# MLP products of a two-layer trunk by Strassen's seven products instead of eight, with the hidden layer kept in DRAM

## The chip, the cores and the metric

The kernel runs on one core of one Trainium2 chip, as one launch. The metric is device microseconds of that core, the median of several runs. An engine name in a profile stands for one of the core's engines: PE is TensorE's matmuls, PEld its weight loads, DVE is VectorE, ACT is ScalarE, POOL is GpSimd, SP is SyncE, which issues most DMAs. "q" behind a name is that engine's instruction queue.

## What is computed

Two layers of a trunk work on 640 tokens (128 context, 512 latent) of 1024 channels in float32. In each layer three branches (a short gated convolution, differential attention, a convolution module) are merged and projected; then comes the squared-ReLU MLP, which this change is about:

```python
    x = x + gt1 * rmsnorm(m @ lw["w_o"], lw["g_post_mix"])
    h = rmsnorm(x, lw["g_pre_mlp"]) * (1 + sc2) + sh2
    f = jnp.square(jax.nn.relu(h @ lw["w_ff1"])) @ lw["w_ff2"]
    x = x + gt2 * rmsnorm(f, lw["g_post_mlp"])
```

w_ff1 is 1024 x 4096 and w_ff2 is 4096 x 1024. Scales and shifts (sh2, sc2, gt2 and their like, six chunks of 1024 a layer) come from w_mod and two conditioning vectors. The outputs are y_prompt, y_sample and the context's new keys and values.

## The kernel before

**Tiles.** Channels stand on the 128 partitions, tokens along the free axis, so an activation is 8 tiles of 128 x 640 and the MLP's hidden layer is 32 of them. `U()` takes a working tile (51 of them, `NU`, each 655 float32 wide), `hl()` two. Tokens are cut into two halves of 320 (`HALF`) or, where one sub-layer ends and the next begins, into parts of 256 and 384 (`PART`).

**Split products.** Every float32 operand is split into a high part, rounded to fp32r, and a low part, the rest. A product is three matmuls: high by high, high by low, low by high. `wblock` loads a block of 128 x 1024 weights (tile `raw`, 3 of them), makes the high part on ACT (`wh`) and the low part (`wl`) by a subtraction that goes to DVE or POOL (`nc.either`); there are 5 such pairs (`NW`). `gemm` issues the three products for both halves of the tokens; `proj` gives them a PSUM tile `pp` of two banks, `proj_half` a tile `ps` of one bank.

**MLP.** The hidden channels come in chunks of 4, 8, 8, 8 and 4 tiles (`CHUNKS`, lines 1387 to 1436). In a chunk every hidden tile is one `proj` over 8 input tiles, then `relu2` (ReLU and square on ACT, square and low part on DVE or POOL); then each of the 8 output tiles is one `proj` over the chunk's tiles, added into `ya` on DVE. The first chunk is started by `first`, part by part of the tokens, inside `tail`, the function that ends a sub-layer; the last chunk is itself the `tail` of the MLP, with the norm and the residual. In layer 0 the loop also steps through `mods`, which makes modulation vectors with `modvec`: one `raw` load and four multiply-and-sum instructions of 128 x 512 on DVE for each of 56 tiles (chunk 5 of layer 0 and all six chunks of layer 1). Layer 0's own chunks 2 to 4 are made during its merge of the branches; layer 1 has nothing of the kind there.

**Order of the work.** The program is first recorded as a list of operations (`Recorder`). `rank` gives each a due time so that TensorE may go on without a pause, `schedule` lists every engine's operations with a cost model (`cost`, `LAT`, `pe_time`), and `emit` issues them in that order; so all instructions of the page carry line 517. Each engine works through its list in order. Tiles are taken from their pools in this order, too.

Of the kernel before, what the change touches and what calls it, by code (L numbers as in the profile page):

```python
# [31 lines left out]
CHUNKS = (4, 8, 8, 8, 4)  # L32
# [65 lines left out]
class View:  # L98
    """A view of a tile: what is done to its access pattern, and the elements that it covers."""
# [70 lines left out]
# microseconds from an operation's end to the start of one that waits for it, by the two engines  # L170
# [15 lines left out]
class Recorder:  # L186
    def __init__(self, nc):
# [6 lines left out]
        # operations for either of two engines  # L194
        self.either = Engine(self, "vector", "gpsimd")

    def cost(self, eng, method, outs, ins, kw, args):
        """microseconds that an engine is held."""
# [5 lines left out]
        if eng == "tensor":  # L204
# [9 lines left out]
            return c / 2400  # L214
# [11 lines left out]
        if eng == "gpsimd":  # L226
            if ALU.pow in (kw.get("op"), kw.get("op1")):
                return 0.1 + m * 0.2
            if method == "memset":
                return 0.1 + m / 900  # L230
            return 0.155 + m * 2.1e-3
        return 0.06

    def add(self, eng, method, args, kw, other=None):
# [9 lines left out]
        if eng == "sync":  # L244
            sz = (outs + ins)[0].shape
            nbytes = 4 * int(np.prod(sz))
# [11 lines left out]
        if nbytes:  # L258
            op.acts = ("dma", nbytes)
        if eng == "scalar":  # L260
# [51 lines left out]
    def rank(self):  # L312
        """priorities: the latest start that lets TensorE go on without a pause, in its order of the program."""
        t = 0.0
        for op in self.ops:
            if op.eng == "tensor":
                op.prio = t
                t += op.cols / 2400
# [12 lines left out]
        for op in reversed(self.ops):  # L331
            d = op.dur
            if op.eng == "sync":
                d = 1.3 + op.acts[1] / 360e3
            for u in op.users:
# [4 lines left out]
    def schedule(self):  # L340
        """the operations in the order of their starts."""
# [17 lines left out]
        # operations that use each tile, to know when it is free  # L359
# [25 lines left out]
        def soon(e, op, start):  # L385
            """whether a late operation should let one go first that is about to be ready."""
# [31 lines left out]
        def pe_time(op, t):  # L418
            """duration on TensorE, whose clock doubles after a tick of enough work."""
            left, w, t0 = op.cols, op.load / op.cols, t  # L420
            while left > 0.5:
                i = int(t / TICK + 1e-9)
                rate = 2400 if busy.get(i - 1, 0) >= BUSY else 1200
# [8 lines left out]
        while len(seq) < n:  # L432
# [48 lines left out]
            if e == "sync":  # L481
                gen[0] = max(start, gen[0]) + 0.65
                dma[0] = max(gen[0] + 0.65, dma[0]) + op.acts[1] / 360e3
                op.end = dma[0]
            else:
# [35 lines left out]
def trunk_kernel(ctx: ExitStack, tc: tile.TileContext, xT, crow, ccol, wmod, wmod0, win, wv, wa, wc, wattn, wo, wff1, wff2,  # L521
# [49 lines left out]
    # ---- constants  # L571
# [12 lines left out]
    # ---- weights  # L584
# [5 lines left out]
    def wblock(src, eng=None):  # L590
        r = raw_load(src)
        wh = wp.tile([P, KD * P], F32R, tag="wh", name=nm("wh"), bufs=NW)
        wl = wp.tile([P, KD * P], F32R, tag="wl", name=nm("wl"), bufs=NW)
# [3 lines left out]

    def gemm(outs, wb, rhs, ks, koff=0):
        """outs: [(psum ap, c0, c1)]; rhs[k] = (hi, lo)."""
# [31 lines left out]
    def first(wbs, rhs, hf):  # L631
        """products of four blocks with one part of the tokens, in step with the tiles of rhs."""
# [21 lines left out]
    def sums(ss, c0, c1, w, pos=None):  # L654
        """sums over channels, tokens on partitions; w: the column of 1/n for the mean."""
# [16 lines left out]
    # ---- per-token statistics: means over channels, or rsqrt of them and eps, to a broadcast  # L672
# [22 lines left out]
    def sq_acc(acc, src, a, b, first):  # L695
        """acc[:, a:b] (+)= src^2"""
# [29 lines left out]
    def residual(xs, m, sq, hf, need, part):  # L726
        """m = xs + m * rstd; returns the squares of the new m."""
# [12 lines left out]

    def split(t, hi, lo, eng=None):
# [3 lines left out]
    # ---- modulation  # L745
# [12 lines left out]
    def cond():  # L758
        """silu of the two conditioning rows, on every partition, in halves."""
# [7 lines left out]
    def modvec(l, st, j, cb):  # L767
        """chunk j of the modulation vectors, a tile at a time."""
# [27 lines left out]
    # ---- start: the first layer's scale and shift a tile at a time, each followed by its products  # L796
# [64 lines left out]
    for l in range(DEPTH):  # L861
# [6 lines left out]
        # ---- Conformer conv branch: gated input, first two channel tiles half by half  # L868
# [55 lines left out]
        # ---- lambda  # L924
# [12 lines left out]
        # ---- attention  # L937
# [38 lines left out]
        def rope(pt, out, scale):  # L976
            """rotary embedding of the latent part of a projection into out; returns the projection."""
# [17 lines left out]
        def k_head(hd):  # L995
            """keys: (high parts twice over the partitions for each map, low parts), and the context's as they are."""
# [12 lines left out]
        def q_head(hd):  # L1009
            """queries, scaled: for each map its high part on its own partitions and the low part on the others."""  # L1010
# [7 lines left out]
        def softmax(S, n, view, s0):  # L1018
            """S: two psum views [q, n keys]; returns s0 * (p0 - lam p1) as a tile, s0 the sum under p0."""
# [17 lines left out]
        def three(out, A, B, start, stop):  # L1037
            """out (+)= A.T @ B from (hi, lo) pairs."""
# [30 lines left out]
        def values(aa, ac, v, vc):  # L1069
            """weights @ v of the latent and the context queries, channels on partitions; s0 times the output."""  # L1070
# [24 lines left out]
        def subln(o, s0, hd):  # L1095
            """the output, and what its queries are to be scaled by: rsqrt of the mean square and eps, times s0."""
# [20 lines left out]
        # ---- short gated conv branch  # L1117
# [69 lines left out]
        # ---- modulation vectors that are needed later  # L1187
        def mods(js):
            if l == 0:
                cb = cond()  # L1190
                for j in js:
                    yield from modvec(l, st[l], j, cb)
# [16 lines left out]
        def pair(wsrc):  # L1209
            """a block holds the products of two channel tiles."""  # L1210
# [19 lines left out]
        # ---- layer norm and silu of the conv branch  # L1230
# [22 lines left out]
        # ---- attention output  # L1253
# [38 lines left out]
        # ---- output projection, residual, second norm  # L1292
# [265 lines left out]
```

## Time and profile before

| | |
|---|---|
| median of 3 runs | 2613.51 us (2612.6 to 2614.75) |
| span of the profiled execution, first to last instruction | 2606.3 us |
| what the median has beyond that span | 7.2 us |
| PE busy, PEld busy | 2527.0 us (97%), 2459.4 us (94%), 17092 instructions each |
| DVE, ACT, POOL busy | 1663.9 (64%), 991.9 (38%), 329.0 us (13%) |
| mean granted TensorE clock | 0.985 |

The profiled execution is known by its span alone. Busy is the union of an engine's instructions. Matmuls are pipelined, so their single durations overlap, and what one costs is read from the distance between starts.

### The profile page before, as it was taken

How to read it: one execution, taken by the hardware profiler on the slowest of the kernel's cores; microseconds unless marked ns; L12 is line 12 of the kernel's file. 1: busy time of each engine (PE TensorE's matmuls, PEld its weight loads, DVE VectorE, ACT ScalarE, POOL GpSimd, SP SyncE). 2: the span in 40 equal slices, each digit the busy share in tenths (PEclk: the TensorE clock that was granted, in tenths of full speed). 3: DMA queues.
4: the chain of work that ended last, by engine and by line, in shares of the span. 5: the costliest groups of instructions: out<-in, count | busy, mean ns of one | idle time of the engine just before them, and what ended most of it. 6: DMA issues, size and time to landing. Idle time of an engine off the chain costs nothing. (4 is left out here: it accounts for less than half of the span.)

```text
span 2606.3 us, 41673 instructions
## 1 busy us (share of the span) xinstructions
PE 2527.0 (97%) x17092; PEld 2459.4 (94%) x17092; DVE 1663.9 (64%) x2807; ACT 991.9 (38%) x1714; POOL 329.0 (13%) x218
## 2 busy tenths in 40 slices
PE   7999999999999999999989999999999999999998
PEld 7988899999999999999989888999999989999998
DVE  7699787954675886775468988787243363333325
ACT  4666553223334432222446566433232343222213
POOL 2122220001201010110012222101010020000001
PEclk9999999999999899999989999999999989999999
DMA  7322222341453554444323212123221322222231
GB/s 268 94 79 67 77 73 79 132 168 66 138 182 110 172 172 146 154 151 134 116 74 92 69 62 81 65 105 120 78 73 66 112 91 81 74 73 77 78 110 46
DMA packets 103779, 273.80 MB, mean 105 GB/s; under 512 B 13012, under 2 KB 35876, under 8 KB 103588
## 3 DMA queue, kind: packets, MB, share of 16 engines
q1 hardware_dynamic: 103588, 271.14, 30.8%
q8 instruction: 134, 2.20, 0.3%
q14 instruction: 57, 0.47, 0.1%
HBM read 244.83 MB, written 17.87 MB: 101 GB/s over the span
## 5 line engine op out<-in xcount | busy, mean ns | idle before, releaser
L517 PE MATMUL pp<-u,wh 128*128 128x320 f32 (+2 forms) x6560 | 1245.7, 310 | 13.9 <-DVE u L517 11.4
L517 PEld LDWEIGHTS pp<-u,wh 128*128 128x128 f32 x6560 | 1034.3, 189 | 17.9 <-DVE u L517 13.9
L517 PE MATMUL pp<-u,wl 128*128 128x320 f32 (+2 forms) x3280 | 764.6, 309 | 0.0
L517 PE MATMUL ps<-u,wh 128*128 128x320 f32 (+2 forms) x2912 | 664.6, 317 | 6.0 <-ACT u L517 5.3
L517 DVE TENSOR_TENSOR wl<-raw,wh 128x1024 fp32r<-128x1024 f32 x265 | 332.7, 1256 | 373.8 <-ACT wh L517 373.4
L517 PEld LDWEIGHTS pp<-u,wl 128*128 128x128 f32 x3280 | 555.6, 189 | 0.0
L517 ACT CAST wh<-raw 128x1024 fp32r<-128x1024 f32 x312 | 326.8, 1049 | 590.2 <-PE pp L517 366.9
L517 PEld LDWEIGHTS ps<-u,wh 128*128 128x128 f32 x2912 | 493.3, 191 | 16.8 <-issue 6.7
L517 PE MATMUL ps<-u,wl 128*128 128x320 f32 (+2 forms) x1456 | 456.7, 314 | 0.0
L517 DVE TENSOR_TENSOR u<-u,u 128x640 fp32r<-128x640 f32 (+8 forms) x356 | 279.4, 794 | 65.7 <-ACT u L517 52.1
L517 PEld LDWEIGHTS ps<-u,wl 128*128 128x128 f32 x1456 | 276.9, 190 | 0.0
L517 ACT ACTIVATE u<-pp 128x640 f32<-128x640 f32 (+3 forms) x124 | 79.8, 649 | 439.1 <-PE pp L517 427.7
L517 DVE CUSTOM_DVE_ANT_0 u<-raw,u 128x512 f32<-128x512 f32 x320 | 227.4, 758 | 27.6 <-DMA raw<-in_wmod_dram 25.8
L517 DVE SCALAR_TENSOR_TENSOR u<-u,par,u 128x640 f32<-128x640 f32 (+16 forms) x272 | 240.2, 891 | 3.8
L517 POOL TENSOR_TENSOR wl<-raw,wh 128x1024 fp32r<-128x1024 f32 x47 | 121.7, 2590 | 494.2 <-ACT wh L517 285.6
L517 DVE TENSOR_TENSOR u<-u,pp 128x640 f32<-128x640 f32 (+2 forms) x60 | 45.2, 754 | 182.3 <-PE pp L517 182.1
L517 ACT CAST u<-u 64x640 fp32r<-64x640 f32 (+1 forms) x152 | 110.4, 727 | 121.3 <-DVE u L517 107.1
L517 ACT ACTIVATE u<-u 128x640 fp32r<-128x640 f32 (+5 forms) x200 | 117.5, 600 | 83.6 <-DVE u L517 67.6
L517 POOL TENSOR_TENSOR u<-u,u 128x384 f32<-128x384 f32 (+4 forms) x59 | 88.7, 1514 | 431.8 <-ACT u L517 227.2
L517 ACT ACTIVATE u<-pp,mx 128x640 f32<-128x640 f32 x128 | 100.9, 793 | 72.4 <-DVE mx L517 72.1
L517 PE MATMUL ps<-wh,u 128*128 128x256 f32 x640 | 122.3, 286 | 1.8 <-ACT vo L517 1.8
L517 DVE TENSOR_TENSOR u<-ps,u 128x512 fp32r<-128x512 f32 (+4 forms) x192 | 92.1, 507 | 45.2 <-PE ps L517 23.1
(91 smaller groups left out, 1839.9 us busy)
## 6 DMA issues: line engine op xcount, KB each, us to landing
raw<-in_wff_dram SPq DMA_DIRECT2D x128, 512.0 KB, 3.3
raw<-in_win_dram SPq DMA_DIRECT2D x120, 512.0 KB, 3.3
raw<-in_wmod_dram SPq DMA_DIRECT2D x80, 512.0 KB, 3.3
u<-in_wmod_dram SPq DMA_DIRECT2D x32, 256.0 KB, 6.0
raw<-in_wv_dram SPq DMA_DIRECT2D x16, 512.0 KB, 3.2
u<-u SPq DMA_DIRECT2D x128, 64.0 KB, 2.0
raw<-in_wattn_dram SPq DMA_DIRECT2D x16, 512.0 KB, 3.2
raw<-in_wo_dram SPq DMA_DIRECT2D x16, 512.0 KB, 3.3
```

The source lines that it names most:

```text
L517: getattr(eng, m)(*[r(v) for v in a], **{x: r(v) for x, v in k.items()})
```

## The change

The first 4 and the last 4 hidden tiles of each layer stay as they were (`FD`, `FE`). The other 28 are made two at a time: two output tiles, pairs of input tiles and two halves of the tokens are a 2 x 2 by 2 x 2 block product, done with seven block products and sums of operands. `wseven` makes the seven weight operands from one or two `raw` blocks: three DVE sums, a high part each on ACT, a low part each by a subtraction on DVE, or, for products 1, 2 and 4 (`ADD`), by a negated copy on ACT onto which POOL's DMA adds the block from DRAM. `sums_of` and `pair_of` make the activations' operands. `seven` runs the products in the order of `ORDER`; bank A takes products 1, 6, 7 and 4 one upon the other, and is read after each, bank C takes 5 and 3, bank B takes 2. All 32 hidden tiles are written to DRAM (`fd`) and read back in groups of 8 (4 pairs) for the second product. The pools change: weights are 10 tiles of one tag (each holds two of 512 columns), two tiles `sum` are new, `NU` goes from 51 to 48. In layer 0's MLP `mods` makes 24 tiles (its chunk 5, layer 1's chunks 1 and 0), in layer 1's MLP 8 (chunk 5); layer 1's chunks 2 to 4 move to its own merge. The cost model's TensorE rate goes from 2400 to 2225 columns a microsecond.

```diff
-CHUNKS = (4, 8, 8, 8, 4)
-NU = 51
-NW = 5
+NU = 48
+NW = 10
 NRAW = 3
+NSUM = 2
+ORDER = (1, 5, 6, 2, 7, 3, 4)
+ADD = (1, 2, 4)
+FD = 4
+FE = 4
+NF = 32
...
+    def wseven(srcs, add):
+        n = len(srcs) * 2 * P
+        rs = [raw_load(x) for x in srcs]
+        ss = [wp.tile([P, KD * P], F32, tag="sum", name=nm("sum"), bufs=NSUM) for _ in srcs]
...
+        w11, w22, w12, w21 = (part(rs, i) for i in range(4))
+        nc.vector.tensor_add(two(ss[0][:, :2 * n]), two(rs[0][:, :2 * n]), w21[:, None, :].to_broadcast([P, 2, n]))
+        s3, s1, s2, s4 = (part(ss, i) for i in range(4))
+        nc.vector.tensor_add(s2, s3, w22)
+        nc.vector.tensor_add(s4, s2, w12)
+        loaded = {1: 0, 4: 1, 2: 2}
+        of = {1: w11, 2: w12, 3: s4, 4: w22, 5: s1, 6: s2, 7: s3}
+        out = {}
+        for i in ORDER:
+            w = wtile()
+            hi, lo = w[:, :n], w[:, n:2 * n]
+            nc.scalar.copy(hi, of[i])
+            if i in add:
+                nc.scalar.mul(lo, of[i], -1.0)
+                nc.gpsimd.dma_start(lo, part(srcs, loaded[i]), accum_op=ALU.add)
+            else:
+                nc.vector.tensor_sub(lo, of[i], f(hi))
+            out[i] = hi, lo
+        return out
...
-    def modulate(x, sq, G, B, h, hf):
+    def modulate(x, sq, G, B, h, hf, keep=None):
...
+                if keep is not None:
+                    nc.scalar.activation(keep[k][:, s:e], t[:, s:e], AF.Identity, bias=B[:, k, g:g + 1])
...
+    def sums_of(x0, x1):
+        ta, tb = U(), U()
+        nc.vector.tensor_sub(ta[:, :TH], x0[:, :TH], x0[:, TH:])
+        nc.vector.tensor_sub(ta[:, TH:], x1[:, TH:], x0[:, TH:])
+        nc.vector.scalar_tensor_tensor(tb[:, :TH], ta[:, :TH], -1.0, x1[:, TH:], op0=ALU.mult, op1=ALU.subtract)
+        nc.vector.scalar_tensor_tensor(tb[:, TH:], tb[:, :TH], -1.0, x1[:, :TH], op0=ALU.mult, op1=ALU.subtract)
+        out = []
+        for t in (ta, tb):
+            th = hl()
+            nc.scalar.copy(th[0], t)
+            nc.vector.tensor_sub(th[1], t, f(th[0]))
+            out.append(th)
+        return out
...
+    def pair_of(x0, x1, h0=None, h1=None):
+        if h0 is None:
+            t = U(F32R)
+            nc.scalar.copy(t[:, :TH], x0[:, :TH])
+            nc.vector.tensor_sub(t[:, TH:], x0[:, :TH], f(t)[:, :TH])
+            x11 = t[:, :TH], t[:, TH:]
+            h1 = hl()
+            nc.scalar.copy(h1[0], x1)
+            nc.vector.tensor_sub(h1[1], x1, f(h1[0]))
...
+    def product(o, i, W, X, start):
...
+            nc.tensor.matmul(o, wh[:, s], hi, start=start and q == 0, stop=False, skip_group_check=True)
+            nc.tensor.matmul(o, wh[:, s], lo, start=False, stop=False, skip_group_check=True)
+            nc.tensor.matmul(o, wl[:, s], hi, start=False, stop=last, skip_group_check=True)
...
+    def seven(W, X, y0, y1, fresh):
+        ac = PP()
+        A, C = ac[:, 0, :TH], ac[:, 1, :TH]
+        B = PS()[:, :TH]
...
+        def put(y, o):
+            if fresh:
+                nc.scalar.copy(y, o)
+            else:
+                nc.vector.tensor_add(y, y, o)
+        product(A, 1, W, X, True)
+        put(y11, A)
+        product(C, 5, W, X, True)
+        put(y22, C)
+        product(A, 6, W, X, False)
+        put(y12, A)
+        product(B, 2, W, X, True)
+        nc.vector.tensor_add(y11, y11, B)
+        product(A, 7, W, X, False)
+        nc.vector.tensor_add(y22, y22, A)
+        product(C, 3, W, X, False)
+        nc.vector.tensor_add(y12, y12, C)
+        product(A, 4, W, X, False)
+        if not fresh:
+            nc.vector.tensor_add(y21, y21, A)
+        return A
...
-        for cx, cn in enumerate(CHUNKS):
...
+        for i in range(FD):
+            t = U()
+            for hf in range(2):
+                a, b = PART[hf]
+                nc.scalar.activation(t[:, a:b], lead[hf][i], AF.Relu)
+            nc.scalar.activation(t, t, AF.Square)
+            nc.sync.dma_start(fd[i], t)
+        X = [pair_of(hv[2 * j], hv[2 * j + 1], h[2 * j], h[2 * j + 1]) for j in range(KD // 2)]
...
+        for mp in range(FD // 2, NF // 2):
+            W = wseven([wff1[l, 2 * mp + u] for u in range(2)], ADD)
+            y0, y1 = U(), U()
+            A = seven(W, X, y0, y1, True)
+            nc.scalar.activation(y0, y0, AF.Relu)
+            nc.scalar.activation(y0, y0, AF.Square)
+            nc.scalar.activation(y1[:, :TH], A, AF.Relu, scale=-1.0)
+            nc.scalar.activation(y1[:, TH:], y1[:, TH:], AF.Relu, scale=-1.0)
+            nc.scalar.activation(y1, y1, AF.Square)
+            nc.sync.dma_start(fd[2 * mp], y0)
+            nc.sync.dma_start(fd[2 * mp + 1], y1)
+            for _ in range(2):
+                next(mv, None)
...
+        ya = [U() for _ in range(KD)]
+        nu = (NF - FE) // 4
+        for u0 in range(0, nu, 2):
+            us = list(range(u0, min(u0 + 2, nu)))
+            X = [load_pair(2 * u + i) for u in us for i in range(2)]
+            for mp in range(KD // 2):
+                W = wseven([wff2[l, u0 * (KD // 2) + mp * len(us) + i] for i in range(len(us))], ADD)
+                A = seven(W, X, ya[2 * mp], ya[2 * mp + 1], u0 == 0)
+                if u0 == 0:
+                    nc.scalar.copy(ya[2 * mp + 1][:, :TH], A)
```

The last four hidden tiles are read back, split, and go through `tail` as before; there every second output tile is held negated, so its add becomes a subtraction. The weights of both products are laid out on the host in the new order of blocks.

## Rows read from the trace of the kernel before

**Rows 1.** The page's first part: busy us, share of the span, instructions.
```profile
PE 2527.0 (97%) x17092; PEld 2459.4 (94%) x17092; DVE 1663.9 (64%) x2807; ACT 991.9 (38%) x1714; POOL 329.0 (13%) x218
```
**Rows 2.** Busy time by stretch: attention, merge, MLP, MLP's end, of both layers.
```profile
core 0: us, PE busy (x) PEld busy (x) DVE busy (x) ACT busy (x) POOL busy (x), PEclk, DMA share, GB/s
54.00:449.00 395.00, 382.16 (x2632) 353.66 (x2631) 321.52 (x529) 218.57 (x444) 77.30 (x48) 1.00 0.24 76
449.00:778.00 329.00, 328.47 (x2253) 328.21 (x2252) 223.78 (x378) 97.45 (x118) 35.72 (x17) 1.00 0.39 136
...
855.00:1240.00 385.00, 383.05 (x2574) 382.08 (x2575) 281.48 (x597) 101.95 (x129) 37.05 (x20) 0.99 0.46 153
...
1340.00:1736.00 396.00, 381.42 (x2569) 352.33 (x2569) 319.16 (x508) 210.18 (x429) 75.16 (x48) 0.99 0.24 77
1736.00:2065.00 329.00, 328.81 (x2258) 328.55 (x2257) 159.72 (x182) 91.89 (x112) 25.98 (x11) 1.00 0.26 88
...
2143.00:2165.00 22.00, 20.05 (x102) 18.69 (x100) 10.56 (x18) 7.72 (x14) 0.35 (x1) 0.86 0.01 2
2165.00:2540.00 375.00, 372.89 (x2539) 372.39 (x2538) 126.56 (x133) 93.53 (x115) 2.24 (x2) 1.00 0.25 84
```
**Rows 3.** Timeline of layer 1's MLP, DVE: start, duration, instruction, idle before.
```profile
2259.16 0.82 DVE L517 TENSOR_TENSOR u<-u,pp 128x640 f32<-128x640 f32 x1 [2.67 <-PE pp L517]
2259.95 1.22 DVE L517 TENSOR_TENSOR wl<-raw,wh 128x1024 fp32r<-128x1024 f32 x1
2266.18 0.82 DVE L517 TENSOR_TENSOR u<-u,pp 128x640 f32<-128x640 f32 x1 [5.00 <-PE pp L517]
```
**Rows 4.** Timeline of PE in a stretch of one-bank products: first and last of 16.
```profile
1740.09 0.45 PE L517 MATMUL ps<-u,wh 128*128 128x320 f32 x2
...
1746.63 0.46 PE L517 MATMUL ps<-u,wh 128*128 128x320 f32 x2
```
**Rows 5.** Timeline of DVE at the head of layer 1's MLP.
```profile
2148.44 3.78 DVE L517 SCALAR_TENSOR_TENSOR u<-u,mod,u 128x384 fp32r<-128x384 f32 x7
2162.62 1.22 DVE L517 TENSOR_TENSOR wl<-raw,wh 128x1024 fp32r<-128x1024 f32 x1 [10.39 <-ACT wh L517]
...
2168.76 1.02 DVE L517 TENSOR_TENSOR u<-u,u 128x384 fp32r<-128x384 f32 x2
2169.70 2.35 DVE L517 TENSOR_TENSOR wl<-raw,wh 128x1024 fp32r<-128x1024 f32 x2
```
**Rows 6.** Timeline of DVE in layer 0's MLP: two of modvec's multiply-and-sum instructions.
```profile
1079.53 0.69 DVE L517 CUSTOM_DVE_ANT_0 u<-raw,u 128x512 f32<-128x512 f32 x1
...
1080.14 0.69 DVE L517 CUSTOM_DVE_ANT_0 u<-raw,u 128x512 f32<-128x512 f32 x1
```
**Rows 7.** Timeline of ACT at the head of layer 1's MLP.
```profile
2164.48 0.85 ACT L517 ACTIVATE u<-ps 128x384 f32<-128x384 f32 x2
2165.22 0.93 ACT L517 ACTIVATE u<-u 128x384 fp32r<-128x384 f32 x2
...
2166.99 1.98 ACT L517 CAST wh<-raw 128x1024 fp32r<-128x1024 f32 x2
```
**Rows 8.** DVE groups by form, whole span: count, busy us, mean ns, idle before.
```profile
L517 DVE TENSOR_TENSOR u<-u,ps 128x320 f32<-128x320 f32 x16 | 6.5, 482 | 5.2 <-PE ps L517 5.2
```
**Rows 9.** What PE waited for, whole span: us in total, times, longest.
```profile
PE ps L517 <- DVE u L517: 32.6, 30, 10.4
PE pp L517 <- DVE u L517: 13.9, 14, 4.3
```
**Rows 10.** DMA issues: count, KB each, median us from issue to landing.
```profile
raw<-in_wff_dram SPq DMA_DIRECT2D x128, 512.0 KB, 3.3
u<-in_wmod_dram SPq DMA_DIRECT2D x32, 256.0 KB, 6.0
...
u<-on SPq DMA_DIRECT2D x16, 320.0 KB, 3.8
```
**Rows 11.** POOL groups by form, whole span.
```profile
L517 POOL TENSOR_TENSOR wl<-raw,wh 128x1024 fp32r<-128x1024 f32 x47 | 121.7, 2590 | 494.2 <-ACT wh L517 285.6 <-DVE u L517 169.6 <-PE ps L517 27.3
```

More of the change, by code (lines that the diff above doesn't have):

```diff
@@ L259, in add @@
             op.acts = ("dma", nbytes)
+            if kw.get("accum_op") is not None:
+                for v in outs:
+                    self.access(op, v, False)
         if eng == "scalar":
@@ L334, in rank @@
                 d = 1.3 + op.acts[1] / 360e3
+            elif op.eng == "gpsimd" and op.acts is not None:
+                d = 3.0 + op.acts[1] / 150e3
             for u in op.users:
@@ L422, in pe_time @@
                 i = int(t / TICK + 1e-9)
-                rate = 2400 if busy.get(i - 1, 0) >= BUSY else 1200
+                rate = 2225 if busy.get(i - 1, 0) >= BUSY else 1112
                 room = ((i + 1) * TICK - t) * rate
@@ L484, in schedule @@
                 op.end = dma[0]
+            elif e == "gpsimd" and op.acts is not None:
+                op.end = start + 3.0 + op.acts[1] / 150e3
             else:
@@ new lines, in halves @@
+    def halves(t):
+        return [tuple(x[:, i * TH:(i + 1) * TH] for x in t) for i in range(2)]
+    def pair_of(x0, x1, h0=None, h1=None):
[8 more added lines that the diff above has]
+        else:
+            x11 = halves(h0)[0]
+        x21, x22 = halves(h1)
+        ta, tb = sums_of(x0, x1)
+        return [x11, x21, x22, *halves(ta), *halves(tb)]
@@ new lines, in trunk_kernel @@
+    OPND = {1: 0, 2: 1, 3: 2, 4: 6, 5: 3, 6: 5, 7: 4}
+    def product(o, i, W, X, start):
+        wh, wl = W[i]
+        for q, x in enumerate(X):
+            s = slice(q * P, (q + 1) * P)
+            hi, lo = x[OPND[i]]
+            last = q == len(X) - 1
+            nc.begin()
+            nc.tensor.matmul(o, wh[:, s], hi, start=start and q == 0, stop=False, skip_group_check=True)
+            nc.tensor.matmul(o, wh[:, s], lo, start=False, stop=False, skip_group_check=True)
+            nc.tensor.matmul(o, wl[:, s], hi, start=False, stop=last, skip_group_check=True)
+            nc.done()
@@ L1188, in mods @@
         def mods(js):
[L1189 to L1192, printed above, removed]
+            cb = cond()
+            for j in js:
+                yield from modvec(l, st[l], j, cb)
         mv = mods((2,))
@@ L1366, in trunk_kernel @@
         xsrc = xnew
+        lead.append(first(wbs, h, 1))
         def mods():
+            cb = cond()
+            yield from modvec(l, st[l], 5, cb)
             if l + 1 < DEPTH:
                 st[l + 1] = load_par(l + 1)
-                cb = cond()
-                yield from modvec(l, st[l], 5, cb)
-                for j in (1, 0, 2, 3, 4, 5):
+                for j in (1, 0):
                     yield from modvec(l + 1, st[l + 1], j, cb)
         mv = mods()
-        ya = [None] * KD
@@ new lines, in trunk_kernel, with load_pair @@
+        fd = [dr.tile([P, T], F32, name=nm("fd")) for _ in range(NF)]
+        for i in range(FD):
[6 more added lines that the diff above has]
+        X = [pair_of(hv[2 * j], hv[2 * j + 1], h[2 * j], h[2 * j + 1]) for j in range(KD // 2)]
+        def load_pair(j):
+            xs = [U() for _ in range(2)]
+            for i in range(2):
+                nc.sync.dma_start(xs[i], fd[2 * j + i])
+            return pair_of(*xs)
@@ new lines, in trunk_kernel @@
+        for _ in mv:
+            pass
+        ya = [U() for _ in range(KD)]
[8 more added lines that the diff above has]
+                    nc.scalar.copy(ya[2 * mp + 1][:, :TH], A)
@@ new lines, in trunk_kernel, with mid @@
+        ff = []
+        for i in range(NF - FE, NF):
+            t = U()
+            nc.sync.dma_start(t, fd[i])
+            th = hl()
+            split(t, *th)
+            ff.append(th)
+        last = l + 1 == DEPTH
+        h = None if last else [hl() for _ in range(KD)]
+        xnew = None if last else [dr.tile([P, T], F32, name=nm("xs")) for _ in range(KD)]
+        lead = []
+        wbs = []
+        def mid():
+            wbs.extend(conv_blocks(l + 1))
+            lead.append(first(wbs, h, 0))
@@ new lines, in trunk_kernel @@
+        for hf, sq, xt in tail(lambda d: wff2[l, NF - FE + d], ff, list(range(FE)), ya, xsrc, der[:, 3], not last,
+                               None if last else mid, *((PARTL, PSEGL) if last else (PART, PSEG))):
+            a, b = (PARTL if last else PART)[hf]
+            if not last:
+                modulate(xt, sq, st[l + 1][2][:, 0], st[l + 1][1][:, 0:KD], h, hf)
+            for k in range(KD):
+                nc.sync.dma_start((yT if last else xnew)[k][:, a:b], xt[k][:, a:b])
+        if not last:
+            lead.append(first(wbs, h, 1))
@@ L1452, in _pairs, with _quads @@
     return b.reshape(-1, 2, P, b.shape[2]).transpose(0, 2, 1, 3).reshape(-1, P, 2 * b.shape[2])
+def _quads(w, n):
+    K, M = w.shape
+    t = w.reshape(K // (n * P), n // 2, 2, P, M // (2 * P), 2, P)
+    b = [t[:, :, k, :, :, m] for k, m in ((0, 0), (1, 1), (1, 0), (0, 1))]
+    b = np.stack(b).transpose(1, 4, 3, 0, 2, 5).reshape(-1, P, n // 4, KD * P)
+    return b.transpose(0, 2, 1, 3).reshape(-1, P, KD * P)
 _DPERM = np.concatenate([np.arange(0, 16), np.arange(32, 48), np.arange(16, 32), np.arange(48, 64)])
@@ L1497, in _layout @@
     out["wo"] = np.stack([_blocks(a["w_o"][l]) for l in range(L)])
-    out["wff1"] = np.stack([_blocks(a["w_ff1"][l]) for l in range(L)])
+    f0, f1 = FD * P, (NF - FE) * P
+    out["wff1"] = np.stack([np.concatenate([_blocks(w[:, :f0]), _quads(w[:, f0:], KD)]) for w in a["w_ff1"]])
     ff2 = []
-    for l in range(L):
-        k0, bl = 0, []
-        for n in CHUNKS:
-            w = a["w_ff2"][l][k0 * P:(k0 + n) * P]
-            bl.append(_blocks(w) if n == KD else _pairs(w))
-            k0 += n
-        ff2.append(np.concatenate(bl))
+    for w in a["w_ff2"]:
+        f8 = f1 // D * D
+        ff2.append(np.concatenate([_quads(w[:f8], KD), _quads(w[f8:f1], KD // 2), _pairs(w[f1:])]))
     out["wff2"] = np.stack(ff2)
```

83 lines of the change are left out of this document (21 added, 62 removed).

## The prediction

> **What bounds the kernel now.** I read the page's busy times first: PE is busy 2527.0 of 2606.3 us and PEld nearly as long, while DVE has 64% and ACT 38% [rows 1]. Then the stretches: in both MLPs PE is idle 2 us of some 380, at full granted clock; DVE is busy 281 us in layer 0's (modulation tiles) and only 127 in layer 1's [rows 2]. Next the distance between matmuls, since their durations overlap. One hidden or output tile is 48 matmuls of 320 columns, and its evictions start at 2259.16 and 2266.18 us [rows 3]: 7.02 us, so 146.3 ns a matmul. Last, what PE waited for: DVE by far the most, nearly all outside the MLP [rows 9, 2]. So TensorE sets the MLP's pace, and a matmul removed there is worth 146 ns as long as the other engines, which get more to do, keep up.
>
> **What is removed.** Per layer and 2 x 2 block of hidden tiles, 96 matmuls become 84 in the first product (14 blocks, minus 168). In the second, 28 hidden tiles x 8 outputs x 2 halves x 3 = 1344 become 14 pairs x 4 x 21 = 1176 (minus 168). Over two layers that is 672. The new products write one bank, three matmuls at a time, where the old ones alternated between two. The trace has such products: 15 triples between 1740.09 and 1746.63 us [rows 4], 145 ns a matmul, so nothing is lost by it. 672 x 146.4 ns = **98.4 us** off PE.
>
> For the same distance the Trainium skill (TensorE: Matmul & The Clock Gate, Back-to-back issue gap) gives columns / 2.4 GHz + 2.5 ns for isolated matmuls, 136 ns here; by that the gain would be an estimated 91 us. The rows show 146, and I stay with them.
>
> **What DVE gets.** Instructions of one engine overlap a little, so I count from start to start. Two 1024-column subtractions take 2.35 us in all with one lasting 1.22, hence 1.13 from start to start; two of 384 take 1.02, hence 0.46 [rows 5]; a line through both gives 0.60 for 512, 0.40 for 320, 0.73 for 640, 0.33 for 256. Seven scalar-tensor-tensors of 384 in 3.78 us [rows 5] give 0.53 each, 0.46 for 320. modvec's 512 take 0.61 [rows 6], 2.45 a tile.
> - A block of weights from two raw tiles (one "quad"): 1.13 + 2 x 0.60 for sums, 4 x 0.60 for low parts = 4.7 us. Its evictions on DVE are 3 x 0.40 in the first product, 7 x 0.40 in the second (3 in the second's first group). PE needs 84 x 0.1464 = 12.3 us for it.
> - First product: 14 quads x 5.9 = 83 us, plus 24 modvec tiles (59 us) in layer 0 or 8 (20 us) in layer 1, against 172 us of PE. DVE is at 82% or 60%.
> - Second product: a pair of hidden tiles read back costs 0.40 + 0.73 + 2 x 0.40 + 2 x 0.46 + 2 x 0.73 = 4.3 us. A full group (4 pairs, 4 quads) costs 4 x 7.5 + 17.3 = 47.4 us on DVE against 49.2 on PE, the first group 41. The last has half as many matmuls, 24.6 us of PE, but DVE needs 4 x (2.6 + 2.8) + 8.7 = 30.3. In sum 166 us of DVE against 172 of PE: this is the place where it can go wrong.
>
> ACT, from 0.93 for a cast of 1024, 0.41 for 384 and 0.37 from PSUM [rows 7], has 8.6 us in a quad of the first product and less in the second; it is at 70% and stays hidden. relu2's DVE work (two instructions of 640 a hidden tile) goes, and the pairs' replaces it.
>
> **What moves.** 24 modvec tiles go to layer 1's merge, 59 us of DVE and 24 loads. DVE has 159.7 of 329 us there; layer 0's merge does the same work with 223.8, and PE is busy 328.5 of 329 in it [rows 2]. I cost that at nothing; PE hides it. The SP queue gets 32 stores and 32 loads of 320 KB a layer; such a load lands in 3.8 us [rows 10], the group that needs it is tens of us away, and the DMA engines are a quarter to a half busy in the MLPs [rows 2]: nothing, unless a load waits for a working tile, next.
>
> **What is added on the path.**
> - Head of the MLP: sums of four pairs, 4 x (0.80 + 0.92 + 1.46) = 12.7 us of DVE, under the first chunk's products, where DVE idles 10.4 us [rows 5]. But that chunk holds 8 of the 10 weight tiles, so the first quad's operands come late. PE idles 2 us there already [rows 2]. Bounds 0 and 12.7; I take 3 a layer: +6.
> - Group changes: four pairs keep 28 working tiles, ya 8, so 12 of 48 are left, enough to prepare one pair ahead and, as the old group's operands come free product by product, about a second. The other two cost 8.7 us of DVE under the first quad. Four changes a layer (the first one from the hidden product), bounds 0 and 8.7 each; I take 3, nearer the lower since products 1 and 5 need only some of the operands: +24.
> - Last group: DVE needs 5.7 us more than PE, twice: +11.4. Bounds: 0 (weights made ahead), and 12 each if instructions cost their full duration.
> - Evictions late while DVE is at 96%: 3 a layer, +6. Layer 0's first product, where three raw tiles serve weights and modvec: +4. Three working tiles fewer in attention, where PE idles 13 to 15 us a layer [rows 2]: +3, bounds 0 and a doubling.
> - The low parts made by POOL's DMA: 256 KB onto SBUF, three a quad. No row shows an accumulating DMA. Below, 512 KB land in 3.3 us; above, 256 KB take 6.0 in the kernel's start [rows 10], and POOL's own slow step of 2.6 us [rows 11] may lie ahead. Ten weight tiles let a product's operands be started up to nine products (15.8 us) ahead, so 4 to 9 us is hidden: 0. Without that cover it would cost its excess over 15.8 us once per ten products, some 39 times.
>
> A sentence apart: the Trainium skill (DMA: Bandwidth & Descriptors, Anatomy of one DMA) has 2.0 us plus bytes / 436 KB per us for a GpSimd DMA, an estimated 2.6 us here; by that, too, the term is nothing.
>
> Sum: 2606.3 - 98.4 + 6 + 24 + 11.4 + 6 + 4 + 3 = 2562.3 us of span. The median lies 7.2 above the span, so **2570 us**.
>
> **Rivals.**
> 1. *All of it hidden.* For it: DVE's average stays under PE's. Against: the last group and the group changes, where it doesn't. 2613.5 - 98.4 = 2515, with the head 2521.
> 2. *DVE sets the second product.* If instructions cost their full durations (1.22 for 1024, 0.48 for an eviction [rows 3, 8]) because they wait for one another, a quad takes 8.8 us, a pair 5.0, a full group 55 against 49, the last 37 against 24.6. That is 24 us a layer where I counted 8.7: 2600. For it: sums and pairs are chains of dependent instructions. Against: the subtractions are independent, and waiting ones can be filled in.
> 3. *Bank A is exposed.* Three times a quad the next product on A has to wait for an eviction, with one product of 12 matmuls (1.76 us) between. The eviction takes 0.48 [rows 8] and may queue behind one instruction of 1.22. If DVE runs behind its list, PE pays: 60 quads x 3 places; at 0.24 us a place (43 us) the gain is gone, at the eviction's whole 0.48 it is 86 us and 2656. Against: the cover is over twice the eviction. The Trainium skill's Perfetto Trace Analysis (Matmuls) speaks for this rival: it wants independent groups to rotate through the banks so that reading one overlaps the next group.
> 4. *The other side: accumulating DMAs are the bound.* If POOL's DMAs pass one after another, p us each, a quad can't take less than 3p, nor a half quad of the last group. 52 full quads of 12.3 us and 8 half ones of 6.15 lose nothing below p = 2.05, 49 us at 4.1, where the gain is gone, and 85 at 4.3: 2655. For it: 256 KB in 6.0 us [rows 10]. Against: that row is from the start, where many loads crowd; the 128 loads of 512 KB in the MLPs take 3.3 at the median.
>
> **Chances.** Mine 0.55, rival 1 0.10, rival 2 0.20, rival 3 0.06, rival 4 0.09. A measurement can tell about 0.2% (5 us) of this kernel from no change. Mine and rival 1 are nearly all faster, rival 2 three times in four, rivals 3 and 4 are slower: faster 0.78, same 0.06, slower 0.16. The range runs from 2530, where nearly three quarters of the 54 us of added terms are hidden, to 2625, past rival 2 with dearer changes; my own case alone is 2545 to 2595.
>
> **What would show it.** PE should have 672 matmuls fewer. In the first product PE should run without gaps, at 12.3 us a quad. In the second, gaps should stand at the four changes of group and in the last group, ended by DVE, and DVE should be busy over 90% there. Layer 1's merge should keep its 329 us. It would be wrong if weight tiles end PE's waits by a DMA from wff (rival 4), if gaps of a few tenths recur at every product (rival 3), or if attention grows by more than some us.

## The result, and the profile after

The changed kernel takes **2771.27 us** (2768.27 to 2776.58, 4 runs) against 2613.06 us for the kernel before on the same chip: a ratio of 1.061 (95% interval 1.060 to 1.063). I had forecast 2570, with a range to 2625. It is 158 us slower, with 672 matmuls fewer.

The page's first part after the change, to be read beside [rows 1]:

```profile
PE 2517.2 (91%) x16420; PEld 2388.3 (86%) x16420; DVE 1929.4 (70%) x3480; ACT 1344.9 (49%) x2518; POOL 492.9 (18%) x397
```

The matmuls are gone as counted, 17092 to 16420. But PE's busy time fell by only 10 us, and its idle time grew from 79 to 255 us. Two things make up most of the difference to the 98 us: a matmul ahead of a stop counts with its own 0.31 us instead of the 0.146 to the next start, and the trace has 317 stops of over 0.05 us where there were 84 (an estimated 38 us); and the mean granted clock is 0.974 instead of 0.985 (an estimated 33 us). No other engine is near full. Busy time by stretch in the changed kernel; the columns are those of [rows 2]. The stretches are attention, merge, and the MLP's first and second product, of layer 0 and then layer 1:

```profile
54.00:473.00 419.00, 398.40 (x2688) 369.63 (x2687) 327.07 (x548) 221.96 (x449) 84.54 (x52) 0.98 0.23 73
473.00:820.00 347.00, 334.56 (x2258) 332.13 (x2257) 215.96 (x365) 95.92 (x119) 48.97 (x22) 0.99 0.38 128
914.00:1086.00 172.00, 140.87 (x875) 130.69 (x874) 124.62 (x290) 105.63 (x204) 28.66 (x34) 0.98 0.86 230
1086.00:1320.00 234.00, 201.48 (x1272) 186.55 (x1271) 174.03 (x315) 138.14 (x254) 38.85 (x45) 1.00 0.70 178
1424.00:1838.00 414.00, 391.96 (x2586) 362.50 (x2587) 321.72 (x514) 214.98 (x437) 84.39 (x52) 0.97 0.23 72
1838.00:2184.00 346.00, 334.60 (x2263) 332.53 (x2263) 215.26 (x366) 95.91 (x119) 49.24 (x22) 0.99 0.38 128
2280.00:2452.00 172.00, 146.25 (x905) 135.32 (x904) 99.53 (x189) 114.89 (x215) 30.28 (x35) 0.98 0.76 203
2452.00:2686.00 234.00, 200.30 (x1247) 185.53 (x1246) 162.50 (x287) 133.12 (x244) 37.98 (x44) 0.99 0.64 161
```

In layer 1's first product PE is idle 26 of 172 us while DVE is busy 58% and ACT 67%: nothing is at its limit, so PE waits for single instructions, not for throughput. And attention and merge, whose code the change hardly touches, are longer: the first load of wa, with which the merge begins, is issued at 472.9 us instead of 449.1.

I cut all runs at the same marks: the first load of wa in each layer, the last broadcast of the norm ahead of the MLP, and the first broadcast at the MLP's end (both are matmuls from tile st). The rest is the program's end and, in layer 0, the MLP's end up to its last group of broadcasts. The stage from one mark to the next, both layers added, in us of the one profiled execution; the kernel before took 2604.6 to 2617.3 us in 25 runs, so differences of a few us in this table say nothing:

| run | attention | merge, output projection | MLP | rest | span |
|---|---|---|---|---|---|
| before | 849.4 | 810.3 | 874.5 | 72.1 | 2606.3 |
| changed | 889.6 | 833.9 | 978.3 | 70.1 | 2771.9 |
| e1: C in its own PSUM tile | 890.0 | 832.9 | 861.1 | 69.8 | 2653.9 |
| e2: before, 48 working tiles | 866.9 | 836.7 | 878.8 | 75.2 | 2657.6 |
| e3: before, planner at 2225 | 888.5 | 812.3 | 875.5 | 66.9 | 2643.2 |
| e4: changed, planner at 2400 | 863.4 | 847.1 | 943.8 | 70.8 | 2725.2 |
| e5: e1 and e4 | 862.9 | 844.8 | 837.1 | 72.5 | 2617.3 |
| e6: e5, loads planned later | 863.0 | 849.8 | 830.5 | 73.5 | 2616.8 |
| e7: e5, no accumulating DMA | 867.1 | 845.3 | 830.5 | 74.5 | 2617.4 |
| e8: e5, 51 working and 8 weight tiles | 876.4 | 803.9 | 834.0 | 70.6 | 2584.9 |
| e9: e8, A and B in one tile | 871.1 | 797.0 | 896.2 | 69.6 | 2634.0 |
| e10: e8, first product without accumulating DMAs | 873.0 | 800.1 | 809.7 | 71.9 | 2554.8 |
| e11: e8, sums in working tiles, 10 weight tiles | 855.4 | 808.8 | 848.1 | 72.6 | 2585.0 |
| e12: e10 and e11 | 846.9 | 806.0 | 818.7 | 76.3 | 2548.0 |

So there are two losses to explain: 104 us in the MLPs, where 98 should have been gained, and 62 us outside them. Together they are 166 us of span; the medians differ by 158.

What the MLP's loss looks like is seen in one quad. The timeline of the changed kernel in layer 1's first product, PE's rows and the evictions of pp that end its stops (start, duration, instruction; in brackets the idle time before and what ended it; other rows of DVE and ACT left out):

```profile
2428.58 1.94 PE L533 MATMUL ps<-u,w 128*128 128x320 f32 x12
2430.35 2.80 PE L533 MATMUL pp<-u,w 128*128 128x320 f32 x18
2433.19 0.49 DVE L533 TENSOR_TENSOR u<-u,pp 128x320 f32<-128x320 f32 x1 [0.80 <-PE pp L533]
2433.73 1.58 PE L533 MATMUL pp<-u,w 128*128 128x320 f32 x9 [0.58 <-DVE u L533]
2435.42 0.49 DVE L533 TENSOR_TENSOR u<-u,pp 128x320 f32<-128x320 f32 x1 [0.74 <-PE pp L533]
2435.96 4.23 PE L533 MATMUL pp<-u,w 128*128 128x320 f32 x27 [0.65 <-DVE u L533]
2440.23 0.42 ACT L533 COPY u<-pp 128x320 f32<-128x320 f32 x1 [0.25 <-PE pp L533]
2440.70 2.03 PE L533 MATMUL pp<-u,w 128*128 128x320 f32 x12 [0.51 <-ACT u L533]
2442.77 0.42 ACT L533 COPY u<-pp 128x320 f32<-128x320 f32 x1 [0.26 <-PE pp L533]
2443.25 1.15 PE L533 MATMUL pp<-u,w 128*128 128x320 f32 x6 [0.52 <-ACT u L533]
2444.23 1.05 PE L533 MATMUL ps<-u,w 128*128 128x320 f32 x6
```

The 12 matmuls of product 2 on bank B (tile ps) start at 2428.58, the next quad's at 2444.23: 15.65 us a quad, where 84 matmuls take 12.3 (the window ends inside the row at 2444.23). In between PE stops four times, and each time the row that ends it is an eviction of tile pp. The first stop tells most. After B come 12 matmuls of product 7 on A and 6 of product 3 on C, 18 in tile pp. The eviction of A could start when the 12 are done; it starts at 2433.19, when all 18 have run, for DVE was idle 0.80 us until then. And the seventh matmul of product 3, on C, which that eviction doesn't read, waits for it. Both directions go through the tile that A and C share.

The instructions in the trace say where these waits come from. The eviction at 2433.19 carries a wait for a semaphore that PE counts up with the 12th and again with the 18th of those matmuls, and it starts 0.04 us after the 18th ends. The weight load of the seventh matmul of product 3 carries a wait for the semaphore that this eviction counts up. So the waits are set in the program. The planner doesn't foresee them: its own dependencies (`access`, `region`) go by columns of a tile, and to it A and C are apart.

### The profile page after: what moved, and what is told of

It reads as the page before. It is cut to its first block, busy times and chain, and to the rows that moved or that the text cites. A ratio compares the mean times of both kernels' runs of the same rounds, so it can differ in the third digit from the quotient of the medians.

```text
span 2771.9 us, 42902 instructions
## 1 busy us (share of the span) xinstructions
PE 2517.2 (91%) x16420; PEld 2388.3 (86%) x16420; DVE 1929.4 (70%) x3480; ACT 1344.9 (49%) x2518; POOL 492.9 (18%) x397
## 4 chain that ended last, share of the span: by engine, by line
PE 36%; DVE 6%; ACT 3%; DMA 2%; issue 2%; POOL 1%; SPq 0%; DVEq 0%; ACTq 0%; POOLq 0%
PE pp L533 21%; PE ps L533 15%; DVE u L533 4%; ACT u L533 2%; DMA raw<-in_wff_dram 1%; ACT w L533 1%; DMA u<-fd 1%; DVE mx L533 0%; POOL u L533 0%; DVE sum L533 0%; POOL w L533 0%; DVE w L533 0%; DVE su L533 0%; DMA raw<-in_wo_dram 0%; ACT pc L533 0%
## 5 line engine op out<-in xcount | busy, mean ns | idle before, releaser
L533 PE MATMUL pp<-u,w 128*128 128x320 f32 (+1 forms) x8496 | 1335.8, 313 | 155.0 <-DVE u L533 100.4
L533 PEld LDWEIGHTS pp<-u,w 128*128 128x128 f32 x8496 | 1252.9, 189 | 217.9 <-DVE u L533 133.2
L533 PE MATMUL ps<-u,w 128*128 128x320 f32 (+2 forms) x5040 | 813.4, 318 | 11.2 <-ACT u L533 5.3
L533 PEld LDWEIGHTS ps<-u,w 128*128 128x128 f32 x5040 | 773.5, 193 | 25.2 <-issue 7.1
L533 ACT CAST w<-raw 128x1024 fp32r<-128x1024 f32 (+2 forms) x380 | 313.8, 828 | 296.9 <-PE ps L533 107.6
L533 DVE TENSOR_TENSOR u<-u,u 128x640 fp32r<-128x640 f32 (+6 forms) x435 | 330.5, 770 | 89.2 <-ACT u L533 77.5
L533 DVE TENSOR_TENSOR w<-raw,w 128x1024 fp32r<-128x1024 f32 x151 | 188.9, 1254 | 169.5 <-ACT w L533 168.4
L533 ACT CAST u<-u 128x640 fp32r<-128x640 f32 (+2 forms) x288 | 199.6, 699 | 164.1 <-DVE u L533 118.2
L533 DVE SCALAR_TENSOR_TENSOR u<-u,par,u 128x640 f32<-128x640 f32 (+14 forms) x272 | 235.9, 900 | 2.4
L533 ACT ACTIVATE u<-u 128x640 f32<-128x640 f32 (+4 forms) x260 | 156.1, 614 | 116.6 <-DVE u L533 92.8
```

The costliest lines, as they stand in the source:

```text
L533: getattr(eng, m)(*[r(v) for v in a], **{x: r(v) for x, v in k.items()})
```

## The experiments

**1. C in a PSUM tile of its own (e1).** The edit to the changed kernel:

```diff
-        A, C = ac[:, 0, :TH], ac[:, 1, :TH]
+        A, C = ac[:, 0, :TH], PS()[:, :TH]
```

> The changed kernel with one edit: bank C gets a PSUM tile of its own (from the one-bank pool) instead of the second bank of A's tile. Theory 1 (the waits of matmuls and evictions go by the PSUM tile, so a read of A holds back the next product on C and the reverse): the quads, 15.6 us apart in the trace of the changed kernel, come down to 12.3 to 13 us; four exposed evictions of 0.8 us a quad go, 52 full quads x 3.3 us and 8 half ones, 170 to 200 us: 2575 to 2605 us in all. Theory 2 (evictions are late because VectorE and ScalarE are behind in their lists): nothing changes in what is queued ahead of an eviction, the quads stay at 15 us or more and the time above 2720 us.

Measured: 2661.3 us, 110 us less than the changed kernel; ratio to before 1.020 (1.018 to 1.022). The MLPs fall from 978.3 to 861.1 us, nothing else moves. The weight loads of product 3 carry no wait for an eviction of A any more (at 2390.80 us, for instance). Theory 1 has the direction and more than half of the size, but not all 170 to 200 us: new gaps of up to 3.1 us came in the place of the old, and the quads of layer 1's first product take 12.3 to 16.9 us, not 12.3 to 13. DVE's timeline there shows one, with PE's row behind it:

```profile
2374.26 0.69 DVE L533 TENSOR_TENSOR w<-sum,w 128x512 fp32r<-128x512 f32 x1
2377.62 1.23 DVE L533 TENSOR_TENSOR sum<-raw,raw 128x1024 f32<-128x1024 f32 x1 [2.67 <-DMA raw<-in_wff_dram]
2378.76 0.48 DVE L533 TENSOR_TENSOR u<-u,ps 128x320 f32<-128x320 f32 x1
2379.16 0.68 DVE L533 TENSOR_TENSOR sum<-sum,raw 128x512 f32<-128x512 f32 x1
2379.76 0.48 DVE L533 TENSOR_TENSOR u<-u,pp 128x320 f32<-128x320 f32 x1
2380.30 3.79 PE L533 MATMUL pp<-u,w 128*128 128x320 f32 x24 [1.47 <-DVE u L533]
```

A sum of weights stands 2.67 us at the head of DVE's list until its load lands. The evictions behind it are late, and PE, which needs A, idles 1.47 us until 2380.30. Whether the order of the list is at fault here, or the load, is asked in e6.

**2. The same wait, half the dose (e9).** On e8 (below, steady quads at 12.3 us), A shares its tile with B instead, and C has its own.

```diff
-        A, C = ac[:, 0, :TH], PS()[:, :TH]
-        B = PS()[:, :TH]
+        A, B = ac[:, 0, :TH], ac[:, 1, :TH]
+        C = PS()[:, :TH]
```

> As the run with 51 working and 8 weight tiles, but now A shares its PSUM tile with B and C has its own. Theory 1 (matmul and eviction wait by the tile): of the changed kernel's four exposed evictions a quad two go and two stay (A is read after product 6 and B's product 2 comes next; B is read after 2 and product 7 on A comes next). So half the cost: about 1.6 us a quad, steady quads at 13.9 us, 60 to 100 us in all on top of 2583. If it was something else about C in that tile (its place, its order), no more than 10 us.

Measured: 2641.2 us against e8's 2583.5, the MLPs 62 us longer, the rest 13 us shorter. PE's timeline in layer 1's first product (here ps is bank C):

```profile
2303.11 3.69 PE L533 MATMUL pp<-u,w 128*128 128x320 f32 x24
2306.63 1.93 PE L533 MATMUL ps<-u,w 128*128 128x320 f32 x12
2308.40 2.79 PE L533 MATMUL pp<-u,w 128*128 128x320 f32 x18
2311.70 1.59 PE L533 MATMUL pp<-u,w 128*128 128x320 f32 x9 [0.52 <-ACT u L533]
2313.87 1.60 PE L533 MATMUL pp<-u,w 128*128 128x320 f32 x9 [0.58 <-DVE u L533]
2315.32 1.93 PE L533 MATMUL ps<-u,w 128*128 128x320 f32 x12
2317.08 3.70 PE L533 MATMUL pp<-u,w 128*128 128x320 f32 x24
```

Two stops instead of four, and 13.97 us from one pair of A products to the next: the 13.9 expected. This settles the MLP's wait: its count follows which products share a tile, with DVE's and ACT's work the same.

**3. The 62 us outside the MLPs (e2, e3, e4).** Two settings of the change act there: 48 working tiles, and the planner's rate. Each alone in the kernel before, and the rate taken back in the changed kernel:

```diff
-NU = 51
+NU = 48
```

> The kernel before with 48 working tiles instead of 51, nothing else. The changed kernel is 60 us longer outside the MLPs (its first merge's weights are asked for at 473 instead of 449 us, for instance). If the three tiles explain that: 2655 to 2680 us, with 20 us more in each attention stage. If they don't (my prediction had 3 us for them): within 10 us of the kernel before.

```diff
-            return c / 2400
+            return c / 2225
...
-                t += op.cols / 2400
+                t += op.cols / 2225
...
-                rate = 2400 if busy.get(i - 1, 0) >= BUSY else 1200
+                rate = 2225 if busy.get(i - 1, 0) >= BUSY else 1112
```

> The kernel before with the planner's TensorE rate of the change (2225 and 1112 columns a microsecond instead of 2400 and 1200), nothing else. If the new order of the instructions explains the 60 us outside the MLPs: 2650 us or more. If the rate only makes the plan truer: 2600 to 2620 us.

e4 takes these same lines back in the changed kernel.

> The changed kernel with the old planner rate (2400 and 1200), nothing else. If the rate costs time outside the MLPs, 2715 to 2745 us, with the first merge's weights asked for at about 450 us; if not, 2760 to 2785 us. The 15.6 us between quads stay by theory 1 in both cases, as the wait isn't one of the plan.

Measured: e2 2654.9 us (ratio 1.017, 1.014 to 1.020), e3 2649.5 (1.015, 1.012 to 1.018), e4 2725.7. Three working tiles cost 44 us, in attention (18, where I expected 20 in each layer) and even more in the merges (26). The rate costs 39 in the kernel before, all in attention. Without it the changed kernel is 46 us shorter, but by the profiled executions 35 of that lie in its MLPs; outside them 50 of the 62 us stay, about what the three tiles cost there in e2 (47). The two settings are not additive: attention has 17 and 39 us from the one and the other, and 40 from both together. That the truer rate only makes the plan truer fell: 2225 columns a microsecond is the truer figure (146.5 ns for 320 columns and the 6 that `cost` adds), yet the plan made with it is worse. In the same stretch of attention, the kernel before (first line) has PE idle 13 of 386 us at a granted clock of 1.00, e3 (second line) 21 us at 0.97:

```profile
54.00:440.00 386.00, 373.16 (x2571) 344.66 (x2570) 312.96 (x519) 215.40 (x440) 77.30 (x48) 1.00 0.24 76
54.00:440.00 386.00, 365.23 (x2455) 334.92 (x2455) 292.71 (x499) 209.38 (x430) 84.79 (x52) 0.97 0.23 71
```

TensorE pauses more, and some 3% of the clock is lost to time at the lower of its two levels (1.2 instead of 2.4 GHz). Why this plan pauses more was not followed further and stays open.

**4. Both edits, and two guesses about what remains (e5, e6, e7).** e5 is e1's and e4's edits together.

> The changed kernel with both edits that helped alone: bank C in a PSUM tile of its own (minus 110 us alone) and the planner's old TensorE rate of 2400 (minus 46 us alone). If the two are independent, 2605 to 2625 us, no change against the kernel before. If the first edit's gain was held down by a plan that is off, less: 2580 or so. What then stays of the 98 us of removed matmuls has gone to the three working tiles (44 us in the kernel before with 48) and to what still stops TensorE in the MLP.

Measured: 2616.0 us, ratio 1.002 (1.000 to 1.004), as the sum of the two says. On it, e6 lets the planner expect loads 1.5 us later:

```diff
-                d = 1.3 + op.acts[1] / 360e3
+                d = 2.8 + op.acts[1] / 360e3
...
-                op.end = dma[0]
+                op.end = dma[0] + 1.5
```

> As the run with both edits, and the planner takes a load to land 1.5 us later (it plans 2.8 us for 512 KB; in the changed kernel the blocks of w_ff land 4.2 us after issue at the median, 3.3 before). Theory A (VectorE's list has a sum of weights ahead of an eviction, the sum waits 2.7 us for its load, and TensorE waits for the eviction behind it): with the sums placed later the gaps of 1.2 to 1.8 us, one a quad in the first product, go: 25 to 45 us less than the run with both edits. Theory B (the load is late because the three raw tiles are held, whatever the list says): within 10 us of it.

Measured: 2615.8 us, no change. The MLPs gained 7 us and attention and merge lost 5. What PE waited for in layer 0's MLP, in e5 and then in e6 (us in total, times, longest):

```profile
PE pp L533 <- ACT u L533: 11.5, 11, 2.7
PE pp L533 <- DVE u L533: 6.5, 6, 1.5
PE pp L533 <- DMA w<-in_wff_dram: 4.9, 5, 1.8
```
```profile
PE pp L533 <- DMA w<-in_wff_dram: 16.2, 10, 4.7
PE pp L533 <- DVE u L533: 2.9, 3, 1.5
PE pp L533 <- ACT u L533: 2.4, 3, 1.0
```

The waits that ACT and DVE end shrink, as theory A would have it, and waits for accumulated low parts come in their place; in layer 1's MLP it is the same (11.4 to 2.7 us, and 2.2 to 9.9). Theory A falls as a way to win time; theory B has the forecast that came true, but that the raw tiles make the load late isn't shown. In e7 VectorE makes all the low parts:

```diff
-ADD = (1, 2, 4)
+ADD = ()
```

> As the run with both edits, but with all seven low parts made by VectorE and no accumulating DMA (ADD empty). Rival 4 of the prediction (accumulating DMAs are a bound) and its milder form (they make the loads land later): faster by 10 us or more, and the blocks of w_ff land in 3.5 us or less. Against it: VectorE gets 1.8 us a quad more, 9.3 of 12.3 us in the second product and with the pairs 55 for 49 us a group, so 30 to 60 us slower.

Measured: 2618.8 us, ratio to before 1.003 (1.002 to 1.005): no real change either, neither the gain nor the loss that was expected. DMA issues (count, KB, median us to landing) of e5 and of e7:

```profile
raw<-in_wff_dram SPq DMA_DIRECT2D x128, 512.0 KB, 5.7
...
w<-in_wff_dram POOLq DMA_DIRECT2D x156, 256.0 KB, 6.0
```
```profile
raw<-in_wff_dram SPq DMA_DIRECT2D x128, 512.0 KB, 3.7
```

The accumulating DMAs aren't a bound, but with them the loads of weights land in 5.7 us instead of 3.7. Without them layer 1's first product runs at 12.3 us a quad nearly throughout. What that gains, the second product loses at its changes of group, where DVE has no room (busy 154 of the last 170 us): there, in layer 1, 84 matmuls take over 19 us twice.

**5. Versions that use this (e8, e10, e11, e12).** e8 takes e5 and pays for 51 working tiles with two weight tiles:

```diff
-NU = 48
-NW = 10
+NU = 51
+NW = 8
```

> As the run with both edits, but 51 working tiles again, paid for with two weight tiles (8 instead of 10, as much memory). If the 48 tiles cost 44 us as in the kernel before, and weights made five to seven products ahead are early enough (an accumulated low part lands 5.5 us after issue, a product takes 1.76 us): 40 us less than the run with both edits, the attention stages back at 449 and 400 us. If ten weight tiles are needed, the MLPs lose what attention gains.

Measured: 2583.5 us, ratio 0.989 (0.987 to 0.992). That is 33 us less than e5, where 40 were expected. The merges are back (803.9 us), attention isn't (876.4): it is 14 us longer than in e5 although it has three working tiles more. e11 tests whether the two weight tiles are missing there. e10 makes low parts by DVE in the first product only:

```diff
-            W = wseven([wff1[l, 2 * mp + u] for u in range(2)], ADD)
+            W = wseven([wff1[l, 2 * mp + u] for u in range(2)], ())
```

> As the run with 51 working and 8 weight tiles; in the MLP's first product alone all low parts are made by VectorE, in the second as before. The run without accumulating DMAs had quads of 12.3 us all through layer 1's first product, but lost it at the second's changes of group (19 us for a quad). If VectorE has room in the first product only: 10 to 20 us less, 2565 to 2575. If the loss of layer 0, where VectorE also has modvec, is as large: no change.

Measured: 2559.4 us, 0.981 (0.979 to 0.983): 24 us less than e8, more than the 10 to 20 expected, all in the MLPs. The edit takes three accumulating DMAs a quad away, and from ACT the three negated copies; which of the two gains the 24 us was not separated. e11 is e8 with the sums in working tiles and ten weight tiles:

```diff
-        ss = [wp.tile([P, KD * P], F32, tag="sum", name=nm("sum"), bufs=NSUM) for _ in srcs]
...
-        nc.vector.tensor_add(two(ss[0][:, :2 * n]), two(rs[0][:, :2 * n]), w21[:, None, :].to_broadcast([P, 2, n]))
-        s3, s1, s2, s4 = (part(ss, i) for i in range(4))
+        s3, s1, s2, s4 = (U(w=n) for _ in range(4))
+        nc.vector.tensor_add(s3, w11, w21)
+        nc.vector.tensor_add(s1, w22, w21)
```

> As the run with 51 working and 8 weight tiles, but the sums of weights live in working tiles (four of 512 columns a quad, no tiles of their own), and the memory goes to 10 weight tiles again. The run with 8 weight tiles has attention stages of 466 and 410 us against 449 and 400 before. If two weight tiles cost that: attention back at 450 and 400, 20 to 27 us less. Against it: four working tiles fewer for preparing pairs, up to 4 us more at each of eight changes of group.

Measured: 2575.8 us, 0.987 (0.985 to 0.989): 8 us under e8 where 20 to 27 were expected. Attention came back by 21 us (855.4) as expected, but the MLPs went up by 14. Some of that may be the profiled execution, which at 2586.7 us was 11 above the run's median; that the MLPs are short of working tiles is a guess that no run tests. e12 is both:

> Both of the two edits above: sums in working tiles with 10 weight tiles, and no accumulating DMA in the first product. If they add up: 2540 to 2555 us, 60 us under the kernel before; what is left of 98 us then lies at the head of the MLP and at changes of group.

Measured: **2553.6 us**, 0.979 (0.977 to 0.980): 55 us under the kernel before, as expected, and the best of these runs. Its steady quad in layer 1's first product:

```profile
2292.16 3.68 PE L532 MATMUL pp<-u,w 128*128 128x320 f32 x24
2295.67 1.90 PE L532 MATMUL ps<-u,w 128*128 128x320 f32 x12
2297.41 1.92 PE L532 MATMUL pp<-u,w 128*128 128x320 f32 x12
...
2304.45 3.68 PE L532 MATMUL pp<-u,w 128*128 128x320 f32 x24
```

Product follows product without a stop, and 12.29 us lie between the first and the last row: the 12.3 that the prediction counted for 84 matmuls.

## Why the prediction was wrong, point by point

**The step that failed** is in rival 3 and in the term for evictions: "Three times a quad the next product on A has to wait for an eviction, with one product of 12 matmuls (1.76 us) between." There was no such cover. A and C were taken from one PSUM tile, and by the program's semaphores matmuls and evictions waited for each other by the tile; so the product that should have hidden an eviction waited for it too. I had 3 us a layer for this, and for the rival at most 0.48 us in three places, with a chance of 0.06. The trace has four places and 15.65 - 12.3 = 3.3 us a quad, 0.8 each: the eviction's 0.49, its start after the last matmul and PE's restart after it. e1 and e9 show it by count, and the sign that I had named for this rival, gaps of a few tenths at every product, was there. Its dearest price (86 us) was too low by half: 52 full quads at 3.3 us are an estimated 172. The diff showed the cause: one `PP()` for A and C. I counted banks where I should have asked what the waits go by. Perfetto Trace Analysis (Matmuls) of the Trainium skill, whose rule I weighed and set aside, asks that independent groups rotate through the banks so that evictions overlap; the runs agree with it (e1: 110 us less), and add that two banks of one tile don't count as two here, at 0.8 us an eviction, since the waits set in this program go by the tile.

**Two costs outside the MLPs.** Three working tiles were put at 3 us, in attention, with a bound of 28; e2 measured 44, more than half of it in the merges, where I expected none. PE was busy 328.5 of 329 us there before, and I took that as a sign of room; with 48 tiles it isn't so. The planner's rate was costed at nothing, without a word; e3 measured 39. Together they are the 62 us: with 51 working tiles, ten weight tiles and the old rate, e12 spends 1729 us outside its MLPs, the kernel before 1732.

**A small term.** I added 7.2 us from span to median. In every run here an execution's time lies 1.7 to 2.2 us above its own span, so some 5 us of the term is an execution that happened to be short, and nothing that the change keeps.

**What held.** The count of matmuls, and their price from one-bank rows: steady quads of 12.3 us in layer 1's first product. The move of 24 modvec tiles into layer 1's merge: with 51 tiles again (e8) both merges together are 804 us against 810 before. The accumulating DMAs: 256 KB land in 5.5 us in the changed kernel, within the 4 to 9 that I allowed, and PE waited once for one, 1.7 us. So rival 4, which named the right side, has the wrong mechanism. But nothing, my price for them, held only while the tile's waits gave them time: PE waits 7.1 us for them in e5 and 26.1 in e6, and without them in the first product e10 is 24 us faster than e8. The Trainium skill's line for a GpSimd DMA (DMA: Bandwidth & Descriptors, Anatomy of one DMA) had given an estimated 2.6 us; an accumulating one beside these loads takes twice that. ScalarE and VectorE have room in layer 1's first product, where e12 keeps 12.3 us a quad; in layer 0's, with modvec, no run does throughout (e12: 12.3 to 16.8).

**The sum for the MLP.** My terms for it were -98.4 + 51.4 = -47 us. With the shared tile gone, the old rate and 51 tiles, the runs measure -40 (e8), -26 (e11), -56 (e12) and -65 (e10). So a few lines turn this kernel into one whose MLPs gain about what I forecast; for the one at hand the forecast was wrong, by the waits of one tile and by two settings. That the sums lie near is partly luck. By 84 matmuls at 12.3 us, the traces have the first products losing 43 us in e8 and 17 in e12, where I had 10 with the heads; the full groups of the second product 21 in both, where I had 30 with late evictions; the last groups 5 and 12, where I had 11.4.

**Open.** Why a truer TensorE rate gives a worse plan of attention, and why three working tiles cost the merges more than attention.

## What to carry to other kernels

Before counting a product as cover for an eviction, ask what the next matmul really waits for: if waits are set by the tile, as in this program, and two accumulators come out of one tile, each read can stop both. A change that takes a few buffers or retunes a planner's constant is costed over the whole program, by a run of the old kernel with that setting alone; here these two cost 44 and 39 us, each by itself, and I had added 51 for the whole new stage. And where PE stops at a fixed beat while no engine is full, read one beat instruction by instruction: the row that ends the gap names the wait.

## What the hardware showed unexpectedly

An accumulating DMA of 256 KB takes 0.86 us of POOL's time to issue and, at the median of a run, lands in 5.5 to 6.1 us. Beside three of them a quad, ordinary loads of 512 KB land in 4.2 to 5.7 us at the median; in e7, without them, in 3.7.
